# Running sums, sums of squares and the last residual's additions moved from GpSimd to VectorE in a two-layer decoder trunk

## The chip, the cores and the metric

The kernel runs on one core of one Trainium2 chip. The metric is the device time of one execution in microseconds (us); the time of a kernel is the median of its runs. The core's engines work side by side: TensorE (PE in the profile, its weight loads PEld) multiplies, VectorE (DVE), ScalarE (ACT) and GpSimd (POOL) work elementwise, and SyncE (SP) issues the transfers. Each engine takes its own instructions in the order in which the program lists them.

## What is computed

A trunk of two layers over 512 tokens of width 1024, in fp32. Cut to what matters here:

```python
def layer_norm(x, g, b):
    mu = jnp.mean(xf, axis=-1, keepdims=True)
    var = jnp.mean(jnp.square(xf - mu), axis=-1, keepdims=True)
    y = (xf - mu) * lax.rsqrt(var + LN_EPS)
    return (y * g + b)

for layer in range(DEPTH):
    if layer % 2 == 0:
        mix = concat([s5_mixer(...), stick_breaking_attention(...)]) @ mix_w_out[i] + mix_b_out[i]
    else:
        # inside: GLU, causal depthwise convolution of width 31, layer_norm, silu, product
        mix = conformer_conv(x, ...)
    x = layer_norm(DEEPNORM_ALPHA * x + mix, ln1_g[layer], ln1_b[layer])
    ffn = sqrelu_mlp(x, ffn_w1[layer], ffn_b1[layer], ffn_w2[layer], ffn_b2[layer])
    x = layer_norm(DEEPNORM_ALPHA * x + ffn, ln2_g[layer], ln2_b[layer])
```

## The kernel before

The activations lie with features on the 128 partitions and tokens along the row: `X[0]` to `X[7]` are eight 128x512 tiles, and a layer norm's mean runs over partitions and tiles. It is therefore a product with a matrix of 1/1024 (`ones`) on TensorE, which leaves the mean on every partition. Each product of activations and weights is made of three passes over two-part splits of both operands (`whi`, `wlo` of the weights, `xh`, `xl` or `hh`, `hl` of the activations): ScalarE rounds the high part (`CAST`, or `ACTIVATE` for a normalised tile), and VectorE subtracts to get the low part (L91 for weights, L198 and L877 for activations).

Four of the layer norms run in this layout, in two halves of 256 tokens each (`HALVES`): norm a (behind the mixer of layer 0), b (behind its feed-forward block), c (inside the convolution module) and d (behind that module). The fifth norm works on transposed tiles and is not touched.

A half goes through these steps. `LN.add` (L833) keeps a running sum `s` over the eight tiles as they come, seven additions of 128x256; those for tiles 1 to 6 are on GpSimd, the one for tile 7 on VectorE. `LN.norm` sends the sum through TensorE (`mp`, L841), subtracts the mean from the eight tiles on VectorE, squares them on ScalarE (`sq`), adds the squares up (tiles 0 to 3 by three additions on GpSimd at L853, tiles 4 to 7 by three on VectorE), and sends both partial sums through TensorE (`vp`). Then come the reciprocal root on ScalarE (`r`) with a refinement on VectorE (`t`), and in `ln_to_x` a scaling of each tile (`X<-X,PV,r`) and its split (`xh` on ScalarE, `xl` on VectorE at L877).

TensorE is given other work meanwhile. `tail_norm_lead` runs the second half's products of the block before (`Tail`, tiles `tla`, `tlb`, `tld`) while the first half is normalised, and the first half's products of the next block (`Lead`, tiles `fl` or `pl`) while the second half is. The lists `BEFORE` and `LEAD` say how many, and `tc.issue_after` pins the `ones` products behind them; the remaining order on each engine comes from a scheduler that places instructions as they become ready in its own estimate. Since TensorE takes its instructions in order, a `vp` product whose operand is late holds up what is listed behind it.

In the convolution module each channel tile's 31 taps are shared: TensorE takes some as diagonal products (`cv`, its diagonals `dh`, `dl` made on ScalarE), VectorE the others as multiply-adds into two accumulators (`cy`, `cz`, L339). The last two channel tiles are worked off in halves of tokens.

Behind norm d the feed-forward block of layer 1 begins: `fl` for its first six hidden tiles, then `f`. Beside it `residual` adds the two split parts of each normalised tile up again (L1098, eight additions of 128x512 on GpSimd), scales them on ScalarE, transposes them on TensorE (`xt`), and the second product of the block (`g`) is added to them.

Of the kernel before, what the change touches and what calls it, by code (L numbers as in the profile page):

```python
# [9 lines left out]
F32 = mybir.dt.float32  # L10
# [3 lines left out]
ALU = mybir.AluOpType  # L14
# [6 lines left out]
KT = D // P  # L21
# [126 lines left out]
def kernel(ctx: ExitStack, tc: tile.TileContext, a: dict, out: bass.AP):  # L148
    nc = tc.nc
    act = Act(tc)  # L150
    V, S, G, PE = nc.vector, nc.scalar, nc.gpsimd, nc.tensor
# [4 lines left out]
    def const(shape, name, dt=F32):  # L156
        return cst.tile(shape, dt, tag=name, name=name)
# [4 lines left out]
    X = [const([P, T], f"X{j}") for j in range(KT)]  # L162
# [28 lines left out]
    def pv(n, i):  # L191
        if n == "mix_b_in":
            return PB[:, i : i + 1]
        return PV[:, vrow[n] + i : vrow[n] + i + 1]
# [38 lines left out]
    def mm(name):  # L233
        return psum("mm", name, MIX_BUFS[0])
# [46 lines left out]
    xs, w0, u0 = [], None, mm("u0")  # L281
# [52 lines left out]
    def tt(o, x, y, op):  # L334
        V.tensor_tensor(o, x, y, op=op)  # L335
        return o
# [365 lines left out]
    ys = []  # L702
# [83 lines left out]
    def nps(name):  # L786
        return nps_.tile([P, T], F32, tag="n", name=name)
# [7 lines left out]
    def tmp(name, dt=F32):  # L795
        return hid.tile([P, T], dt, tag="tmp", name=name, bufs=8)
# [25 lines left out]
    class LN:  # L822
# [5 lines left out]
        def add(self, j, ys, c0, c1):  # L828

            if j == 1:  # L830
                self.s[c0] = tmp(f"s{self.n}{c0}")[:, c0:c1]
            if j:
                (V if j == KT - 1 else G).tensor_tensor(self.s[c0], ys[0][:, c0:c1] if j == 1 else self.s[c0], ys[j][:, c0:c1], op=ALU.add)  # L833

        def colmean(self, srcs, c0, c1, nm, other):

# [7 lines left out]
        def norm(self, ys, c0, c1, others=(None, None)):  # L844

            mu = self.colmean([self.s[c0]], c0, c1, "m", others[0])
            sq = []
            for j, y in enumerate(ys):
                tt(y[:, c0:c1], y[:, c0:c1], mu, ALU.subtract)
                sq.append(tmp(f"sq{self.n}{c0}{j}")[:, c0:c1])  # L850
                act(sq[j], y[:, c0:c1], AF.Square)
            for j in (1, 2, 3):
                G.tensor_tensor(sq[0], sq[0], sq[j], op=ALU.add)  # L853
            tt(sq[4], sq[4], sq[5], ALU.add)
            tt(sq[6], sq[6], sq[7], ALU.add)
            tt(sq[4], sq[4], sq[6], ALU.add)
            var = self.colmean([sq[0], sq[4]], c0, c1, "v", others[1])
            r, t_ = tmp(f"r{self.n}{c0}")[:, c0:c1], tmp(f"t{self.n}{c0}")[:, c0:c1]
            rsqrt(r, t_, var)
            return r  # L860

    def rsqrt(r, t_, var):

        act(r, var, AF.Abs_reciprocal_sqrt, bias=eps_c)
        stt(t_, var, EPS, r, ALU.add, ALU.mult)
        tt(t_, t_, r, ALU.mult)
        stt(r, t_, -3.0, r, ALU.add, ALU.mult)
# [68 lines left out]
    def tail_norm_lead(xk, name, bias, g, b, lead_n, lead_name):  # L936

        ln = LN(name)
        t = Tail(xk, ln, bias)
        t.run(KT)  # L940
        xs = new_x(f"x{name}")
        lead = Lead(lead_n, xs, lead_name)
        ln_to_x(ln, *HALVES[0], g, b, xs, [lambda n=n: t.run(n) for n in BEFORE[:2]])
        t.run(2 * KT - t.done)
        ln_to_x(ln, *HALVES[1], g, b, xs, [lambda n=n: lead.run(n) for n in BEFORE[2:]])
        return xs, lead.finish()
# [25 lines left out]
    xs, first = tail_norm_lead(cat[4:8], "a", rb[0], ("ln1_g", 0), ("ln1_b", 0), LEAD, "fl0")  # L972
# [19 lines left out]
    xs, first = tail_norm_lead(hs, "b", rb[1], ("ln2_g", 0), ("ln2_b", 0), 4, "pl")  # L992
# [75 lines left out]
    for c0, c1 in HALVES:  # L1068
# [8 lines left out]
        ys = [x[0] for x in acc]  # L1077
# [13 lines left out]
    xs, first = tail_norm_lead(cs_, "d", None, ("ln1_g", 8), ("ln1_b", 8), LEAD, "fl1")  # L1091
# [3 lines left out]

    def residual():
        for j in range(KT):
            G.tensor_tensor(X[j], xs[j][0].bitcast(F32), xs[j][1].bitcast(F32), op=ALU.add)  # L1098
            act(X[j], X[j], AF.Identity, bias=pv("ffn_b2", 8 + j), scale=ALPHA)
        for f in range(2):  # L1100
            pss = [nps(f"xt{b}{f}") for b in range(4)]
            for b in range(4):
                for i in range(4):
                    PE.transpose(pss[b][:, i * P : (i + 1) * P], X[4 * f + i][:, b * P : (b + 1) * P], ident)
            for b in range(4):
                XT[2 * b + f] = X[4 * f + b]
                S.copy(X[4 * f + b], pss[b])
# [10 lines left out]
    for bi, nb in enumerate(FFN_BLOCKS[1]):  # L1118
        hs = ffn1(1, bi, k0, nb, xs, stp, first if bi == 0 else ())
        if bi == 0:  # L1120
            residual()
        if bi < len(FFN_BLOCKS[1]) - 1:
            for f in range(2):
                pss = [nps(f"g{bi}{f}{b}") for b in range(4)]
                for k in range(0, nb, 2):
                    wh, wl = W.next()
                    for b in range(4):
                        for kk in range(2):
                            hh, hl = (t_[:, b * P : (b + 1) * P] for t_ in hs[k + kk])
                            for i, (u, v) in enumerate(((hh, wh), (hl, wh), (hh, wl))):  # L1130
                                PE.matmul(pss[b], u, v[:, kk, :], start=k + kk == 0 and i == 0,  # L1131
                                          stop=k + kk == nb - 1 and i == 2)
                for b in range(4):
                    tt(XT[2 * b + f], XT[2 * b + f], pss[b], ALU.add)
        k0 += nb
# [65 lines left out]
```

## Time and profile before

| | before |
|---|---|
| median of 3 runs | 1237.97 us (1237.91 to 1237.98) |
| profiled execution | 1239.18 us, of which the span of its instructions 1237.40 us |
| TensorE busy | 1195.6 us (97% of the span) |
| VectorE busy | 779.3 us (63%) |
| ScalarE busy | 567.1 us (46%) |
| GpSimd busy | 107.1 us (9%) |

All times below count from the start of the span. Norm a lies at 255 to 303 us, norm b at 592 to 660, the convolution module at 650 to 843 with norm c from 791 on, and norm d at 820 to 889. A busy TensorE is not TensorE at its peak, since its matmuls overlap; what it loses shows in the steps between their starts, in its waits and in the granted clock (PEclk).

### The profile page before, as it was taken

Reading aid. Unit: us, or ns where it says so; the run is one execution under the profiler, and the core shown is the slowest. Engines: PE = TensorE matmul, PEld = TensorE weight load, DVE = VectorE, ACT = ScalarE, POOL = GpSimd, SP = SyncE. Lnnn points to the kernel's source line nnn. Section 1 sums busy time; section 2 is a strip of 40 time slices with the busy share of each in tenths; the row PEclk is TensorE's granted clock in tenths of the full one; section 3 lists DMA queues with packets and bytes.
Section 4 is the critical chain, followed back from the end, with each engine's and each line's share of the span. In section 5 each row is a group of like instructions: output and inputs, shape, how many; then the busy total and the mean of one; then the engine's idle time right before and its main releaser. Section 6 shows DMA issues by size and latency. Waiting matters only on the chain.

```text
span 1237.4 us, 16678 instructions
## 1 busy us (share of the span) xinstructions
PE 1195.6 (97%) x6559; PEld 1015.3 (82%) x6559; DVE 779.3 (63%) x1321; ACT 567.1 (46%) x1020; POOL 107.1 (9%) x145
## 2 busy tenths in 40 slices
PE   9899999999999999999999999699899999999997
PEld 7776777789888888888998889689898888888885
DVE  8998774578633434434398999999853443434446
ACT  7736575635523324224255766876562332323230
POOL 1001100131000000000140011123400000000000
PEclk9999999999999999999999999889899999999999
DMA  8510141241533223333133121012052232423211
GB/s 206 162 37 20 35 119 52 85 137 42 163 102 102 80 90 102 102 102 98 43 103 103 35 69 35 1 48 90 33 172 69 85 119 68 134 68 105 86 51 68
DMA packets 111662, 105.93 MB, mean 86 GB/s; under 512 B 9378, under 2 KB 99746, under 8 KB 111584
## 3 DMA queue, kind: packets, MB, share of 16 engines
q1 hardware_dynamic: 111424, 104.84, 27.0%
q8 instruction: 51, 0.84, 0.3%
q14 instruction: 27, 0.22, 0.1%
q10 hardware_dynamic: 160, 0.03, 0.0%
HBM read 100.66 MB, written 4.19 MB: 85 GB/s over the span
## 4 chain that ended last, share of the span: by engine, by line
PE 75%; DVE 16%; ACT 4%; DMA 3%; issue 2%; POOL 1%; DVEq 0%; SPq 0%; ACTq 0%; POOLq 0%
PE f L207 23%; PE g L1131 12%; PE acf L207 11%; PE fl L207 4%; PE h L1115 3%; PE tld L207 3%; DVE cz L339 3%; PE tlb L207 2%; PE cv L1030 2%; DVE wlo L91 2%; DVE cy L339 2%; PE pl L207 1%; PE pv L207 1%; PE pg L207 1%; DVE X L339 1%
## 5 line engine op out<-in xcount | busy, mean ns | idle before, releaser
L90 ACT CAST whi<-raw 128x1024 fp32r<-128x1024 f32 x176 | 183.9, 1049 | 396.9 <-PE f L207 112.1
L91 DVE TENSOR_TENSOR wlo<-raw,whi 128x1024 fp32r<-128x1024 f32 x176 | 219.4, 1251 | 221.7 <-ACT whi L90 221.1
L1131 PE MATMUL g<-whi,hh 128*128 128x512 f32 x208 | 81.5, 392 | 0.0
L1131 PE MATMUL g<-wlo,hh 128*128 128x512 f32 x208 | 81.5, 392 | 0.0
L1131 PE MATMUL g<-whi,hl 128*128 128x512 f32 x208 | 81.4, 391 | 0.0
L207 PE MATMUL f<-xdh,whi 128*128 128x512 f32 x208 | 80.9, 389 | 0.0
L207 PE MATMUL f<-xah,whi 128*128 128x512 f32 x208 | 80.9, 389 | 0.0
L207 PE MATMUL f<-xal,whi 128*128 128x512 f32 x208 | 80.9, 389 | 0.0
L207 PE MATMUL f<-xdh,wlo 128*128 128x512 f32 x208 | 80.9, 389 | 0.0
L207 PE MATMUL f<-xdl,whi 128*128 128x512 f32 x208 | 80.9, 389 | 0.0
L207 PE MATMUL f<-xah,wlo 128*128 128x512 f32 x208 | 80.9, 389 | 0.0
L207 PE MATMUL acf<-hl,whi 128*128 128x512 f32 x192 | 75.2, 392 | 0.0
L207 PE MATMUL acf<-hh,whi 128*128 128x512 f32 x192 | 74.9, 390 | 0.0
L207 PE MATMUL acf<-hh,wlo 128*128 128x512 f32 x192 | 74.7, 389 | 0.0
L197 ACT CAST hh<-fr 128x512 fp32r<-128x512 f32 x64 | 39.7, 621 | 71.7 <-DVE fr L335 71.5
L198 DVE TENSOR_TENSOR hl<-fr,hh 128x512 fp32r<-128x512 f32 x64 | 44.2, 691 | 37.3 <-ACT hh L197 37.2
L339 DVE SCALAR_TENSOR_TENSOR cy<-hp,wdw,cy 128x512 f32<-128x512 f32 (+1 forms) x91 | 60.9, 678 | 0.1
L339 DVE SCALAR_TENSOR_TENSOR cz<-hp,wdw,cz 128x512 f32<-128x512 f32 (+1 forms) x86 | 59.9, 700 | 0.0
L1030 PE MATMUL cv<-hph,dh 128*128 128x256 f32 (+1 forms) x113 | 39.9, 353 | 10.0 <-ACT hph L197 8.3
L335 DVE TENSOR_TENSOR fr<-fr 128x512 f32<-128x512 f32 x64 | 43.8, 686 | 5.4 <-ACT fr L136 5.4
L1131 PEld LDWEIGHTS g<-whi,hl 128*128 128x128 f32 x208 | 39.1, 188 | 8.6
L1131 PEld LDWEIGHTS g<-wlo,hh 128*128 128x128 f32 x208 | 39.1, 188 | 8.6
(684 smaller groups left out, 3168.4 us busy)
## 6 DMA issues: line engine op xcount, KB each, us to landing
raw<-in_ffn_w_dram SPq DMA_DIRECT2D x48, 1024.0 KB, 5.4
raw<-in_ffn_w_dram SPq DMA_DIRECT2D x32, 512.0 KB, 3.5
raw<-in_conv_w_pw_dram SPq DMA_DIRECT2D x12, 1024.0 KB, 5.4
raw<-in_mix_w_in_dram SPq DMA_DIRECT2D x16, 512.0 KB, 4.0
xin<-in_x_dram SPq DMA_DIRECT2D x8, 256.0 KB, 4.1
raw<-in_s_w_glu_dram SPq DMA_DIRECT2D x4, 512.0 KB
raw<-in_mix_w_out_dram SPq DMA_DIRECT2D x4, 512.0 KB
raw<-in_mix_w_out_dram SPq DMA_DIRECT2D x2, 1024.0 KB
```

The source lines that it names most:

```text
L90: i0 = nc.scalar.copy(hi, raw).ins
L91: i1 = nc.vector.tensor_sub(lo, raw, hi.bitcast(F32)).ins
L197: i0 = S.copy(hi, src).ins
L198: i1 = V.tensor_sub(lo, src, hi.bitcast(F32)).ins
L207: ins = PE.matmul(ps[:, c0:c1], u[:, k, ksl], v[:, c0:c1], start=start and k == 0 and i == 0, stop=stop and k == n - 1 and i == 2).ins
L335: V.tensor_tensor(o, x, y, op=op)
L339: V.scalar_tensor_tensor(o, x, s, y, op0=op0, op1=op1)
L1030: PE.matmul(cps[j][:, c0:c1], u, v[:, t + c0 : t + c1], start=t == 0 and i == 0, stop=t == n - 1 and i == 2)
L1115: PE.matmul(ps, u, v, start=k == 0 and i == 0, stop=k == nk - 1 and i == 2)
L1131: PE.matmul(pss[b], u, v[:, kk, :], start=k + kk == 0 and i == 0, stop=k + kk == nb - 1 and i == 2)
```

## The change

The running sums are added on VectorE throughout. The squares are added in four pairs on VectorE, and all four results go through the `ones` product, where two did. The residual's eight additions are on VectorE. `tt` is the helper for a `tensor_tensor` on VectorE (its instructions stand under L335). Nothing else is edited; the scheduler's order follows.

```diff
@@ -830,7 +830,7 @@
             if j == 1:
                 self.s[c0] = tmp(f"s{self.n}{c0}")[:, c0:c1]
             if j:
-                (V if j == KT - 1 else G).tensor_tensor(self.s[c0], ys[0][:, c0:c1] if j == 1 else self.s[c0], ys[j][:, c0:c1], op=ALU.add)
+                tt(self.s[c0], ys[0][:, c0:c1] if j == 1 else self.s[c0], ys[j][:, c0:c1], ALU.add)
 
         def colmean(self, srcs, c0, c1, nm, other):
 
@@ -849,12 +849,9 @@
                 tt(y[:, c0:c1], y[:, c0:c1], mu, ALU.subtract)
                 sq.append(tmp(f"sq{self.n}{c0}{j}")[:, c0:c1])
                 act(sq[j], y[:, c0:c1], AF.Square)
-            for j in (1, 2, 3):
-                G.tensor_tensor(sq[0], sq[0], sq[j], op=ALU.add)
-            tt(sq[4], sq[4], sq[5], ALU.add)
-            tt(sq[6], sq[6], sq[7], ALU.add)
-            tt(sq[4], sq[4], sq[6], ALU.add)
-            var = self.colmean([sq[0], sq[4]], c0, c1, "v", others[1])
+            for j in range(0, KT, 2):
+                tt(sq[j], sq[j], sq[j + 1], ALU.add)
+            var = self.colmean(sq[::2], c0, c1, "v", others[1])
             r, t_ = tmp(f"r{self.n}{c0}")[:, c0:c1], tmp(f"t{self.n}{c0}")[:, c0:c1]
             rsqrt(r, t_, var)
             return r
@@ -1095,7 +1092,7 @@
 
     def residual():
         for j in range(KT):
-            G.tensor_tensor(X[j], xs[j][0].bitcast(F32), xs[j][1].bitcast(F32), op=ALU.add)
+            tt(X[j], xs[j][0].bitcast(F32), xs[j][1].bitcast(F32), ALU.add)
             act(X[j], X[j], AF.Identity, bias=pv("ffn_b2", 8 + j), scale=ALPHA)
         for f in range(2):
             pss = [nps(f"xt{b}{f}") for b in range(4)]
```

The first place is VectorE behind the second half of norm d. `rd` is the reciprocal root, `xdh` and `xdl` are the split parts, `X_61` to `X_68` the eight tiles. Before, the end of its scaling and splitting reads:

```order
L339 SCALAR_TENSOR_TENSOR X_66<-X_66,PV,rd_8432 128x256
L339 SCALAR_TENSOR_TENSOR X_67<-X_67,PV,rd_8432 128x256
L339 SCALAR_TENSOR_TENSOR X_68<-X_68,PV,rd_8432 128x256
L877 SCALAR_TENSOR_TENSOR xdl_8031<-X_64,PV,xdh_8030 128x256
L877 SCALAR_TENSOR_TENSOR xdl_8033<-X_65,PV,xdh_8032 128x256
L877 SCALAR_TENSOR_TENSOR xdl_8035<-X_66,PV,xdh_8034 128x256
L877 SCALAR_TENSOR_TENSOR xdl_8037<-X_67,PV,xdh_8036 128x256
L877 SCALAR_TENSOR_TENSOR xdl_8039<-X_68,PV,xdh_8038 128x256
L91 TENSOR_TENSOR wlo_8513<-raw_7802,whi_8512 128x1024
```

With the change the same place reads:

```order
L874 SCALAR_TENSOR_TENSOR xdl_8031<-X_64,PV,xdh_8030 128x256
L874 SCALAR_TENSOR_TENSOR xdl_8033<-X_65,PV,xdh_8032 128x256
L874 SCALAR_TENSOR_TENSOR xdl_8035<-X_66,PV,xdh_8034 128x256
L339 SCALAR_TENSOR_TENSOR X_67<-X_67,PV,rd_8432 128x256
L339 SCALAR_TENSOR_TENSOR X_68<-X_68,PV,rd_8432 128x256
L335 TENSOR_TENSOR X_61<-xdh_8024,xdl_8025 128x512
L874 SCALAR_TENSOR_TENSOR xdl_8037<-X_67,PV,xdh_8036 128x256
L874 SCALAR_TENSOR_TENSOR xdl_8039<-X_68,PV,xdh_8038 128x256
L335 TENSOR_TENSOR X_62<-xdh_8026,xdl_8027 128x512
L91 TENSOR_TENSOR wlo_8513<-raw_7802,whi_8512 128x1024
```

The first residual addition (`X_61`) now stands ahead of the last two splits, the second right behind them; the other six are listed later, in pairs behind the first three `fr` squarings of the feed-forward block. The last five splits no longer wait behind all the scalings.

The second place is VectorE in the second half of norm c, between the subtraction of the mean and the refinement, as a piece of the difference.

```order
+L335 TENSOR_TENSOR sqc_7690<-sqc_7690,sqc_7693 128x256
+L335 TENSOR_TENSOR sqc_7696<-sqc_7696,sqc_7699 128x256
 L335 TENSOR_TENSOR sqc_7702<-sqc_7702,sqc_7705 128x256
-L91 TENSOR_TENSOR wlo_7765<-raw_7762,whi_7764 128x1024
 L335 TENSOR_TENSOR sqc_7708<-sqc_7708,sqc_7711 128x256
 L91 TENSOR_TENSOR wlo_7769<-raw_7762,whi_7768 128x1024
-L335 TENSOR_TENSOR sqc_7702<-sqc_7702,sqc_7708 128x256
 L91 TENSOR_TENSOR wlo_7775<-raw_7772,whi_7774 128x1024
```

The four pair sums stand together, ahead of the weights' low parts (`wlo`) between which the three additions of before were spread.

The third place is TensorE at the variance of the second half of norm b; `pl` is the next block's first product. Before:

```order
L207 MATMUL pl_5808<-xbl_5444,whi_5199 128x256
L207 MATMUL pl_5808<-xbh_5443,wlo_5200 128x256
L841 MATMUL vpb_5833<-sqb_5754,ones 128x256
L841 MATMUL vpb_5833<-sqb_5766,ones 128x256
L207 MATMUL pl_5866<-xbh_5429,whi_5203 128x256
L207 MATMUL pl_5866<-xbl_5430,whi_5203 128x256
```

With the change:

```order
L207 MATMUL pl_5806<-xbh_5443,wlo_5200 128x256
L841 MATMUL vpb_5831<-sqb_5754,ones 128x256
L841 MATMUL vpb_5831<-sqb_5760,ones 128x256
L841 MATMUL vpb_5831<-sqb_5766,ones 128x256
L841 MATMUL vpb_5831<-sqb_5772,ones 128x256
L207 MATMUL pl_5866<-xbh_5429,whi_5203 128x256
```

Four `ones` products stand where two stood; in norms a and c, where the two stood apart, the four stand together too, or with one product between the last two (first half of c).

## Rows read from the trace of the kernel before

**Rows 1.** The page: busy time and instructions of engines; granted clock in 40 slices.

```profile
PE 1195.6 (97%) x6559; PEld 1015.3 (82%) x6559; DVE 779.3 (63%) x1321; ACT 567.1 (46%) x1020; POOL 107.1 (9%) x145
...
DVE  8998774578633434434398999999853443434446
...
PEclk9999999999999999999999999889899999999999
```

**Rows 2.** Busy time of each engine in four stretches, with clock (PEclk) and transfers.

```profile
254.00:302.00 48.00, 45.09 (x353) 43.56 (x353) 38.91 (x84) 19.39 (x40) 14.50 (x18) 1.00 0.24 77
...
715.00:780.00 65.00, 65.00 (x411) 58.76 (x410) 64.90 (x98) 46.06 (x131) 11.99 (x10) 1.00 0.15 49
...
780.00:806.00 26.00, 14.86 (x78) 12.99 (x77) 25.39 (x66) 21.81 (x61) 3.77 (x5) 0.77 0.00 1
...
881.00:891.00 10.00, 5.62 (x23) 4.63 (x24) 10.00 (x12) 6.44 (x11) 8.06 (x6) 0.75 0.00 0
```

**Rows 3.** The chain that ended last, around two second halves: start, length, what.

```profile
296.12 1.28 DVE X L339 x3
...
319.09 10.91 PE f L207 x48
...
876.11 1.28 DVE X L339 x3
...
908.33 10.91 PE f L207 x48
```

**Rows 4.** Timeline of VectorE behind the last layer norm: start, length, instruction.

```profile
877.30 2.31 DVE L877 SCALAR_TENSOR_TENSOR xdl<-X,PV,xdh 128x256 fp32r<-128x256 f32 x3
...
879.53 4.11 DVE L339 SCALAR_TENSOR_TENSOR X<-X,PV,rd 128x256 f32<-128x256 f32 x5
...
883.57 5.14 DVE L877 SCALAR_TENSOR_TENSOR xdl<-X,PV,xdh 128x256 fp32r<-128x256 f32 x5
```

**Rows 5.** Timeline of GpSimd: a running sum, then the residual additions.

```profile
778.88 1.73 POOL L833 TENSOR_TENSOR sc<-sc,cy 128x256 f32<-128x256 f32 x2 [9.32 <-DVE cy L335]
...
877.86 4.31 POOL L1098 TENSOR_TENSOR X<-xdh,xdl 128x512 f32<-128x512 f32 x3 [6.61 <-DVE xdl L877]
...
884.12 7.95 POOL L1098 TENSOR_TENSOR X<-xdh,xdl 128x512 f32<-128x512 f32 x5 [1.94 <-DVE xdl L877]
```

**Rows 6.** Timeline of VectorE: the convolution's taps.

```profile
722.54 1.23 DVE L339 SCALAR_TENSOR_TENSOR cy<-hp,wdw,cy 128x512 f32<-128x512 f32 x1
...
780.81 0.47 DVE L339 SCALAR_TENSOR_TENSOR cz<-hp,wdw,cz 128x256 f32<-128x256 f32 x1
...
810.67 0.97 DVE L339 SCALAR_TENSOR_TENSOR cz<-hp,wdw,cz 128x256 f32<-128x256 f32 x1
```

**Rows 7.** Timeline of VectorE: six additions or products of SBUF tiles in a row.

```profile
803.29 2.08 DVE L335 TENSOR_TENSOR cy<-cy,rc 128x256 f32<-128x256 f32 x6
```

**Rows 8.** Timeline of TensorE around variance products (two rows each, 128x256).

```profile
650.27 0.28 PE L207 MATMUL pl<-xbh,wlo 128*128 128x256 f32 x1
...
650.39 1.02 PE L841 MATMUL vpb<-sqb,ones 128*128 128x256 f32 x4
...
651.37 0.28 PE L207 MATMUL pl<-xbl,whi 128*128 128x256 f32 x1
...
825.44 0.70 PE L841 MATMUL vpc<-sqc,ones 128*128 128x256 f32 x2 [1.09 <-POOL sqc L853]
```

**Rows 9.** Waits of TensorE from 254 to 925 us: sum, times, longest.

```profile
PE fl L207 <- DVE xdl L877: 3.4, 4, 1.7
...
PE vpa L841 <- POOL sqa L853: 1.4, 2, 1.1
...
PE vpc L841 <- POOL sqc L853: 1.1, 1, 1.1
...
PE vpc L841 <- DVE sqc L335: 0.8, 1, 0.8
...
PE mpb L841 <- DVE sb L833: 0.6, 1, 0.6
```

## The prediction

> **What bounds the kernel now.** I read the page first: TensorE is busy for 97% of the span, VectorE for 63% and GpSimd for 9%; but VectorE's slices stand at 8 or 9 from about 620 to 900 us, and the granted clock leaves its full level only in three slices of the same stretch [rows 1]. So TensorE sets the end, and where it is not full, VectorE does. The busy times by stretch show where. From 715 to 780 us VectorE is busy for 64.90 of 65.00 us; from 780 to 806, still full (25.39 of 26), it leaves TensorE with 14.86 of 26; from 881 to 891 it is busy for all 10.00, TensorE for 5.62, at a clock of 0.75. In norm a (254 to 302) VectorE has 38.91 of 48 [rows 2]. TensorE's waits name the same places: 3.4 us for the low parts behind norm d (`xdl`), 1.4 for `sqa` and 1.1 for `sqc` on GpSimd, 0.8 for `sqc` on VectorE, 0.6 for `sb` [rows 9].
>
> The third view explains VectorE's long instructions. Behind norm d, eight scalings and eight splits of 128x256 take from 876.11 to 888.71 us: five scalings 4.11 us, five splits 5.14 [rows 3, 4]. In the same stretch GpSimd has its eight residual additions, 4.31 us for three and 7.95 for five [rows 5]. In the taps, an instruction of 0.47 us lasts 0.97 when GpSimd adds a running sum beside it [rows 5, 6]. So an addition on GpSimd is not free for VectorE: one of 128x256 lengthens a VectorE instruction by 0.5 us (0.97 less 0.47), one of 128x512 by about 1 us (five splits in 5.14 us, so 1.03 each, against 0.4 from start to start where three scalings take 1.28 [rows 3]). On VectorE itself an addition of 128x256 costs 2.08/6 = 0.35 us [rows 7]. The trade is 0.5 for 0.35 wherever VectorE is full.
>
> The Trainium skill's page "GPSIMD Engine Reference" (Specifications) says that GpSimd's way into SBUF is shared with VectorE and contended by VectorE instructions with two SBUF inputs. The lengthened splits and taps, with two such inputs, agree; the page gives no price.
>
> **The change, part by part.** VectorE takes 6 more sums and 1 more square addition in each of 8 halves, 56 of 128x256 (56 x 0.35 = 19.6 us), and 8 residual additions of 128x512, at most 2 x 0.35 = 0.7 us each (5.6 us). GpSimd stops altogether in these stages. What this does to the end depends on the stage.
>
> 1. The residual. From the second half's first scaling to the start of the first `f` product, norm d takes 908.33 - 876.11 = 32.22 us, norm a 319.09 - 296.12 = 22.97 [rows 3]. The two stretches have the same work, but for a lead of 72 products still listed behind the variance in d and 60 in a; at 0.12 us a product (650.27 to 650.39 [rows 8]) that is 1.4 us. In a, GpSimd is silent there. So its residual costs 32.22 - 22.97 - 1.4 = 7.8 us, part in VectorE's pace, part in the clock of 0.75 that follows TensorE's idling. Against this, one addition now stands ahead of the last two splits (0.7 us on a path of which TensorE still holds some cover): I count 0.3. Term: -7.5. Bounds: if the clock's share stays, only VectorE's own lengthening, 12.6 us less 16 x 0.4 = 6.2, less 0.7, that is -5.5; at most the whole difference, -9.2. The other six additions lie between squarings of the next block, where `f` is 16 us away.
>
> 2. The convolution and norm c. From 722.54 to 810.67 us twelve instructions are lengthened (the first and the last in [rows 6]), 12 x 0.5 = 6.0 us. In exchange come 12 sums and one square addition, 13 x 0.35 = 4.6. VectorE is full: -1.4. In the first half the last square addition no longer sits between taps, and with TensorE idle around it [rows 2] I count -0.7 (0 to -1.4). In the second half TensorE's waits of 1.1 + 0.8 us for the squares go [rows 9], since the four additions now stand together ahead of the weights' low parts; that chain then reaches the next product earlier too. I take -2.5 (bounds -1 to -3.5). Together -4.6.
>
> 3. Norms a and b. The waits of 1.4 and 0.6 us [rows 9] go for the most part; the queue takes 28 additions, in a on a VectorE that has 9 us free of 48 [rows 2], in b partly between products that it waits for anyway. I take -2.5 (+1 if the queue eats the gain, -3.5 if the first half's variance is also earlier).
>
> 4. Norm d ahead of its residual. TensorE waits there for nothing now, and 14 additions (4.9 us) replace lengthenings of some 3 us (about six of 0.5, at the price of rows 6): +0.6 (0 to +1.9).
>
> 5. Variance products. Two more per half. A group of two costs 651.37 - 650.27 less two steps of 0.12 = 0.86 us, and the second product of it takes half the 0.67 us between the group and the row behind it, 0.34 [rows 8]. Two more are +0.67 where the pair stood together (b, d), and less, about +0.47, where two groups of one become one group (a, c): 4 x 0.67 + 4 x 0.47 = 4.6. One of the latter falls on an idle TensorE (first half of c [rows 2]): +4.1 (3.1 to 5.4).
>
> Sum: -7.5 - 4.6 - 2.5 + 0.6 + 4.1 = -9.9 us. The profiled execution took 1239.18 us, 1.78 around its span of 1237.40, and is 1.2 us above the median of the runs; it would take 1229.3. For the median I predict 1237.97 - 9.9 = **1228 us**.
>
> **Rivals.**
>
> *The gain is given back in the same queue.* If TensorE waits for `f`'s weights or the hidden tiles because the residual additions stand ahead of them on VectorE, six of 0.7 us, 4.2 us, return: 1232. Against it: VectorE has 16 us from the last split to the first `f`, and its load there falls by the lengthened `wlo`.
>
> *More than the sum.* If norm c's chain, norms a and b and the clock all reach their good bounds (-9.2 - 6.3 - 3.5 + 4.1), it is 1223. For it: the waits of rows 9 are lower bounds, as a late product delays what follows.
>
> *Slower: VectorE becomes the bound.* If the long instructions are not GpSimd's doing and stay, all 64 additions come on top. In the full stretch from 715 to 811 us that is 13 x 0.35 = 4.6, in norms a, b and d, close to full, perhaps half of 42 x 0.35 = 14.7, so 7.4, behind norm d 0.7, and the products of step 5: 4.6 + 7.4 + 0.7 + 4.1 = +16.8, so 1255. It decides as soon as an addition on GpSimd lengthens VectorE by less than the 0.35 that it saves. Against it: each lengthened row of 4 and 6 lies beside a GpSimd row, and the same stretch behind norm a, without GpSimd, is 7.8 us shorter (step 1).
>
> [...]
>
> *No change to speak of.* The products of step 5 (4.1) and 1.5 us in the queues of norms a, b and d could meet a residual worth only 5.5 and a norm c worth 2: 1238 - 5.5 - 2 + 4.1 + 1.5 = 1236.
>
> **How the numbers follow.** Forecast 0.62 (1225 to 1231), given back 0.15, more 0.13, no change 0.06, slower 0.04. For the range I leave out the last two cases and the outer parts of the two next to the forecast: 1223 to 1234. A measurement of this kernel tells about 0.2% (2.5 us) from no change; so faster (under 1235.5) 0.90, same 0.06, slower 0.04.
>
> **What the profile after would show.** Step 1: eight scalings and eight splits behind norm d in about 7 us, no wait for `xdl` over 1 us, and a granted clock of 1.0 from 880 to 900 us. Step 2: no tap of 128x256 over 0.5 us, and no wait for `sqc` over 0.5. Step 3: no wait for `sqa` or `sb`. Step 5: eight groups of eight `ones` rows. GpSimd's last instruction lies before 250 us. I am wrong if VectorE's additions cost over 0.5 us each, if taps stay long without GpSimd, or if the scheduler's order makes TensorE wait at a new place, most likely where norm d's first half meets a full VectorE.

## The result, and the profile after

The changed kernel takes 1228.65 us (1227.07 to 1229.86, 4 runs), the kernel before 1237.94 beside it: a ratio of 0.9925, 95% interval 0.9908 to 0.9942. Measured again later (x9 below) it was 0.9928 (0.9914 to 0.9941). The profiled execution took 1229.86 us with a span of 1226.3.

The page after, busy time of engines, VectorE's slices and granted clock, to be read against [rows 1]:

```profile
PE 1194.0 (97%) x6591; PEld 1015.1 (83%) x6591; DVE 777.8 (63%) x1385; ACT 565.9 (46%) x1020; POOL 26.4 (2%) x65
...
DVE  7998774588634434434488999999762443434446
...
PEclk9999999999999999999999999899999999999998
```

VectorE has 64 instructions more and is busy 1.5 us less. From slice to slice its load has hardly changed. The clock leaves its full level in one slice of the stretch from 620 to 900 us instead of three. The stretches of [rows 2], by busy time of each engine in windows (PE, PEld, DVE, ACT, POOL, clock, transfers):

```profile
254.00:302.00 48.00, 47.22 (x372) 46.33 (x373) 42.52 (x99) 20.07 (x41) 0.00 (x0) 1.00 0.24 75
715.00:780.00 65.00, 65.00 (x416) 59.00 (x415) 64.23 (x109) 46.44 (x135) 0.00 (x0) 1.00 0.14 46
780.00:806.00 26.00, 15.51 (x85) 13.52 (x84) 25.52 (x70) 22.74 (x63) 0.00 (x0) 0.82 0.00 1
881.00:891.00 10.00, 10.00 (x86) 10.00 (x85) 8.47 (x11) 7.56 (x12) 0.00 (x0) 1.00 0.48 157
```

From 881 to 891 us TensorE is busy throughout at full clock, where it had 5.62 of 10 us at 0.75. From 780 to 806 little has changed: VectorE is still full, and TensorE stands for 7.8 us in a wait for ScalarE's `hph` (8.3 before), which ScalarE makes from VectorE's `hp`. What has changed in the convolution is the longest tap (shortest, middle and longest in ns, from 715 to 815 us), before and after:

```profile
L339 DVE SCALAR_TENSOR_TENSOR cz<-hp,wdw,cz x64: 469/744/1236, 715.5 to 814.7; 128x512 f32<-128x512 f32 x39, 128x256 f32<-128x256 f32 x25
...
L339 DVE SCALAR_TENSOR_TENSOR cz<-hp,wdw,cz x66: 478/745/764, 714.5 to 814.5; 128x512 f32<-128x512 f32 x39, 128x256 f32<-128x256 f32 x27
```

Before, eleven taps of `cy` and `cz` took 0.94 to 1.24 us, each beside an addition on GpSimd; after, none of 128x512 takes over 0.76 and none of 128x256 over 0.50. Next VectorE's timeline behind norm d (start, length, instruction), against [rows 4]:

```profile
871.94 1.28 DVE L339 SCALAR_TENSOR_TENSOR X<-X,PV,rd 128x256 f32<-128x256 f32 x3
873.13 1.27 DVE L874 SCALAR_TENSOR_TENSOR xdl<-X,PV,xdh 128x256 fp32r<-128x256 f32 x3
874.32 1.27 DVE L339 SCALAR_TENSOR_TENSOR X<-X,PV,rd 128x256 f32<-128x256 f32 x3
875.51 1.28 DVE L874 SCALAR_TENSOR_TENSOR xdl<-X,PV,xdh 128x256 fp32r<-128x256 f32 x3
876.70 0.88 DVE L339 SCALAR_TENSOR_TENSOR X<-X,PV,rd 128x256 f32<-128x256 f32 x2
877.49 0.69 DVE L335 TENSOR_TENSOR X<-xdh,xdl 128x512 f32<-128x512 f32 x1
878.09 0.88 DVE L874 SCALAR_TENSOR_TENSOR xdl<-X,PV,xdh 128x256 fp32r<-128x256 f32 x2
```

Eight scalings, eight splits and the first residual addition take 7.03 us (871.94 to 878.97), where scalings and splits took 12.60. The chain that ended last has no VectorE row there any more (against [rows 3]):

```profile
870.02 26.28 PE fl L207 x216
896.30 10.91 PE f L207 x48
907.21 3.56 PE xt L1101 x32
```

From the first scaling to `f` it is now 896.30 - 871.94 = 24.36 us, against 32.22 before. The waits of [rows 9] are gone but for 0.2 us of `vpc`; TensorE's longest ones from 254 to 925 us are now these (sum, times, longest). They are not new: before, the first stood at 8.3 us, one for `dh` in place of `dl` at 1.8, and the third at 0.9.

```profile
PE cv L1027 <- ACT hph L197: 7.8, 1, 7.8
...
PE cv L1027 <- ACT dl L136: 1.4, 1, 1.4
...
PE tla L207 <- ACT whi L90: 0.9, 1, 0.9
```

What has become longer is the variance products. TensorE's timeline in norm d's second half, against [rows 8]:

```profile
868.13 1.89 PE L841 MATMUL vpd<-sqd,ones 128*128 128x256 f32 x8
869.67 0.47 PE L207 MATMUL fl<-xdh,whi 128*128 128x256 f32 x1
```

From the group's start to the next row it is 1.54 us; before, at the same place, 0.67 (873.02 to 873.69).

Where the 11.1 us between the two spans came from shows in the starts of the same rows in TensorE's two timelines. TensorE's work left behind the two rows of variance products is nearly the same: 267 `tld` products behind that of c before and 264 after, and 216 `fl` products between that of d and the first `f` in both.

| place | before | after | shift |
|---|---|---|---|
| first `tla` (norm a begins) | 254.94 | 254.69 | -0.25 |
| first `f` behind norm a | 318.93 | 317.41 | -1.52 |
| first `cv` (behind norm b) | 666.41 | 665.32 | -1.09 |
| first `tld` (behind the first half of c) | 805.42 | 803.13 | -2.29 |
| variance products of c, second half, done | 829.76 | 825.08 | -4.68 |
| variance products of d, second half, done | 873.69 | 869.67 | -4.02 |
| first `f` behind norm d | 908.16 | 896.14 | -12.02 |
| first `h` | 1196.17 | 1184.22 | -11.95 |
| end of the span | 1237.40 | 1226.30 | -11.10 |

Most of it, 8.0 us, comes at one place, behind norm d; 3.6 in the convolution and norm c; norm a gives 1.3, norm b loses 0.4, and norm d ahead of its residual loses 0.7.

### The profile page after: what moved, and what is told of

It is laid out like the page before. It is cut to its first block, busy times and chain, and to the rows that moved or that the text cites. A ratio compares the mean times of both kernels' runs of the same rounds, so it can differ in the third digit from the quotient of the medians.

```text
span 1226.3 us, 16644 instructions
## 1 busy us (share of the span) xinstructions
PE 1194.0 (97%) x6591; PEld 1015.1 (83%) x6591; DVE 777.8 (63%) x1385; ACT 565.9 (46%) x1020; POOL 26.4 (2%) x65
## 4 chain that ended last, share of the span: by engine, by line
PE 81%; DVE 11%; ACT 4%; DMA 3%; issue 1%; POOL 0%; DVEq 0%; SPq 0%; POOLq 0%; ACTq 0%
PE f L207 23%; PE g L1128 12%; PE acf L207 11%; PE fl L207 6%; PE tld L207 4%; PE tlb L207 4%; PE cv L1027 3%; PE h L1112 3%; PE pv L207 2%; PE pg L207 2%; PE pl L207 2%; DVE cz L339 2%; DMA raw<-in_mix_w_in_dram 2%; PE acmo L207 1%; PE av L691 1%; DVE cy L339 1%
## 5 line engine op out<-in xcount | busy, mean ns | idle before, releaser
L91 DVE TENSOR_TENSOR wlo<-raw,whi 128x1024 fp32r<-128x1024 f32 x176 | 214.6, 1224 | 220.2 <-ACT whi L90 218.7
L339 DVE SCALAR_TENSOR_TENSOR cz<-hp,wdw,cz 128x512 f32<-128x512 f32 (+1 forms) x86 | 57.1, 666 | 0.0
L335 DVE TENSOR_TENSOR fr<-fr 128x512 f32<-128x512 f32 x64 | 43.7, 685 | 5.4 <-ACT fr L136 5.4
L1128 PEld LDWEIGHTS g<-whi,hh 128*128 128x128 f32 x208 | 39.1, 188 | 8.5
```

What stands on the lines that cost most here:

```text
L91: i1 = nc.vector.tensor_sub(lo, raw, hi.bitcast(F32)).ins
L339: V.scalar_tensor_tensor(o, x, s, y, op0=op0, op1=op1)
```

## The experiments

The theory: GpSimd's additions lengthen VectorE's instructions beside them; behind norm d this stands on the path to TensorE, in the norms and the convolution less so; and the two more products are a price of their own. The rivals are named with each run.

| run | median, us | ratio to before, interval | first scaling of d to `f`, us |
|---|---|---|---|
| before | 1238.63 / 1238.42 / 1237.73 (beside x1 to x4, x5 to x8, x9 to x11) | | 32.22 |
| x9, the changed kernel again | 1228.82 | 0.9928 (0.9914 to 0.9941) | 24.36 |
| x1, residual only | 1230.19 | 0.9942 (0.9928 to 0.9955) | 24.36 |
| x2, all but the residual | 1234.98 | 0.9973 (0.9964 to 0.9982) | 31.41 |
| x3, residual on GpSimd, late | 1236.83 | 0.9986 (0.9977 to 0.9994) | 25.07 |
| x4, additions beside the splits | 1236.22 | 0.9982 (0.9973 to 0.9991) | 32.64 |
| x5, squares to two | 1225.40 | 0.9893 (0.9877 to 0.9909) | |
| x10, squares to two, again | 1225.61 | 0.9901 (0.9887 to 0.9914) | |
| x6, squares to one | 1231.14 | 0.9942 (0.9929 to 0.9955) | |
| x7, running sums only | 1236.54 | 0.9985 (0.9976 to 0.9995) | 32.00 |
| x8, squares only | 1236.58 | 0.9984 (0.9976 to 0.9993) | 31.45 |
| x11, squares to two, four in c | 1223.98 | 0.9887 (0.9873 to 0.9900) | |

The medians of the three sessions are best compared by their ratios to before. The last column is read as in the prediction's step 1. The lead behind the variance is 72 products in these rows; in x5, x6, x10 and x11 it differs, so they have none.

**x1 and x2: the residual apart from the rest.** x1 is the kernel before with this edit alone; x2 is the changed kernel with it undone.

```diff
-            G.tensor_tensor(X[j], xs[j][0].bitcast(F32), xs[j][1].bitcast(F32), op=ALU.add)
+            tt(X[j], xs[j][0].bitcast(F32), xs[j][1].bitcast(F32), ALU.add)
```

> The kernel before, with only the eight residual additions moved to VectorE. In the changed kernel the stretch from the last variance product of norm d to the first f product is 8.0 us shorter. Theory (GpSimd's additions lengthen VectorE's splits behind norm d, and TensorE waits for these): nearly all of this comes back with this one line, so about 1230 us (1229 to 1231.5), eight scalings and eight splits in about 7 us, and everything ahead of norm d's variance as before. Rival (the gain comes from the running sums and squares, which let norm d begin earlier with more lead left): this line alone gives less than 4 us, so over 1234.

> The changed kernel with the eight residual additions back on GpSimd; running sums and squares stay on VectorE. Theory: the residual's 8 us is lost again, of which nothing depends on the other two parts: about 1236 us (1234.5 to 1237), with lengthened splits behind norm d. Rival (the parts do not add up, since the sums and squares have already freed the stretch): under 1233.

Both came out as the theory had it. In x1 the chain that ended last reads as in the changed kernel, with nothing else of the change in place:

```profile
872.24 26.42 PE fl L207 x216
898.66 10.91 PE f L207 x48
```

From its first scaling at 874.30 that is 24.36 us, to the hundredth the changed kernel's. In x2 the stretch is 31.41. The parts add up within their intervals: 1 - 0.9942 and 1 - 0.9973 make 0.85%, the whole change gave 0.75%.

**x3: the same additions on GpSimd, but behind the splits.** Is it that GpSimd is slow, or that it works beside the splits?

```diff
-        for j in range(KT):
-            G.tensor_tensor(X[j], xs[j][0].bitcast(F32), xs[j][1].bitcast(F32), op=ALU.add)
+        last = None
+        for j in reversed(range(KT)):
+            ins = G.tensor_tensor(X[j], xs[j][0].bitcast(F32), xs[j][1].bitcast(F32), op=ALU.add).ins
+            if last:
+                tc.add_manual_dep(ins, last, NOSYNC, reason="behind the last split")
+            last = ins.name
```

> The kernel before, its residual still on GpSimd, but in reversed order of tiles, so that all eight additions come behind the last split of norm d; everything else as before. Theory (what costs is that the additions lie beside the splits): the eight scalings and eight splits take about 7 us, not 12.6, no wait for the last split over 1 us, and some 6 to 8 us are gained although GpSimd does the same eight additions: 1230 to 1232. The additions then lengthen low parts of weights and squarings, which nothing waits for. Rival (GpSimd is too slow for the residual, wherever it lies, or TensorE's clock falls for another reason): 1236 to 1239, since the additions end some 6 us later still.

The mechanism came out; the time, 1236.83, did not, and lies in the rival's range. VectorE's timeline:

```profile
877.27 1.28 DVE L339 SCALAR_TENSOR_TENSOR X<-X,PV,rd 128x256 f32<-128x256 f32 x3
...
880.84 1.27 DVE L877 SCALAR_TENSOR_TENSOR xdl<-X,PV,xdh 128x256 fp32r<-128x256 f32 x3
...
883.08 0.88 DVE L877 SCALAR_TENSOR_TENSOR xdl<-X,PV,xdh 128x256 fp32r<-128x256 f32 x2 [0.18 <-ACT xdh L136]
884.42 6.48 DVE L91 TENSOR_TENSOR wlo<-raw,whi 128x1024 fp32r<-128x1024 f32 x3 [0.45 <-ACT whi L90]
890.82 1.78 DVE L335 TENSOR_TENSOR fr<-fr 128x512 f32<-128x512 f32 x1
```

and GpSimd's:

```profile
884.05 15.36 POOL L1099 TENSOR_TENSOR X<-xdh,xdl 128x512 f32<-128x512 f32 x8 [11.63 <-DVE xdl L877]
```

Scalings and splits are done in 6.7 us, and `f` starts 25.07 us behind the first scaling (at 902.17 in the timeline; the chain puts a run of `f` 0.17 later, as with 896.14 and 896.30 above). So 7.15 of the 7.86 us are won with GpSimd still adding. But the lengthening has moved to what comes next: three low parts of weights take 6.48 us, in x1 3.49, and a squaring 1.78 instead of 0.68. I had written that nothing waits for these. The chain that ended last says otherwise:

```profile
886.35 4.54 DVE wlo L91 x2
...
906.89 4.66 DMA raw<-in_ffn_w_dram
911.63 1.06 ACT whi L90
912.71 1.24 DVE wlo L91
913.97 3.55 DMA raw<-in_ffn_w_dram
...
919.78 1.14 PE xt L1108 x8
920.92 45.60 PE g L1135 x192
```

By this chain a late `wlo` frees its `raw` buffer late, so the next weights land late; ScalarE waits for them in its queue, and behind them stand the copies of `xt` that TensorE needs to go on. ScalarE's timeline adds a wait for GpSimd's late result in the same queue:

```profile
889.84 0.73 ACT L136 ACTIVATE X<-X,PV 128x512 f32<-128x512 f32 x1 [1.51 <-POOL X L1099]
```

No run tells the share of this wait, which is the rival's lateness, from that of the lengthened `wlo`. Among TensorE's waits from 895 us on:

```profile
PE xt L1108 <- ACT X L1111: 3.9, 1, 3.9
```

From 918 to 925 us its granted clock is 0.76, a mean of its two levels, behind that idle time, and the first block of `g` takes 45.60 us, where x1 has 43.94. 3.9 + 1.66 = 5.6 us go back. So the rival is wrong about the splits and the clock behind norm d (1.00 from 870 to 900 us), and I was wrong that GpSimd's additions would be free anywhere in this stretch.

**x4: GpSimd's additions put back as work that nobody reads.**

```diff
+        du = hpage("du", F32)
         for j in range(KT):
+            G.tensor_tensor(du, xs[j][0].bitcast(F32), xs[j][1].bitcast(F32), op=ALU.add)
             tt(X[j], xs[j][0].bitcast(F32), xs[j][1].bitcast(F32), ALU.add)
```

> The changed kernel, with eight additions of the same operands on GpSimd besides, into a scratch tile that nothing reads (work added, the result is not touched). Theory (an addition on GpSimd lengthens VectorE's instructions beside it): splits of about 1 us and scalings of over 0.4 us return behind norm d, and with them 5 to 8 us: 1234 to 1237. Rival (it was the lateness of the residual's results, or the order of VectorE's instructions): no change from the changed kernel, 1227 to 1230.

1236.22, a ratio of 0.9982 where the changed kernel has 0.9928 (x9): 0.54%, 6.7 us of the gain, are given back. VectorE's timeline, with the same order of instructions as above:

```profile
873.95 2.31 DVE L874 SCALAR_TENSOR_TENSOR xdl<-X,PV,xdh 128x256 fp32r<-128x256 f32 x3
876.18 3.32 DVE L339 SCALAR_TENSOR_TENSOR X<-X,PV,rd 128x256 f32<-128x256 f32 x3
879.42 2.29 DVE L874 SCALAR_TENSOR_TENSOR xdl<-X,PV,xdh 128x256 fp32r<-128x256 f32 x3
881.63 2.90 DVE L339 SCALAR_TENSOR_TENSOR X<-X,PV,rd 128x256 f32<-128x256 f32 x2
```

GpSimd's timeline in the same stretch:

```profile
874.56 4.26 POOL L1096 TENSOR_TENSOR du<-xdh,xdl 128x512 f32<-128x512 f32 x3 [634.84 <-DVE xdl L874]
880.03 4.21 POOL L1096 TENSOR_TENSOR du<-xdh,xdl 128x512 f32<-128x512 f32 x3 [1.22 <-DVE xdl L874]
```

Since nothing reads `du`, lateness and order are ruled out: what costs is that the addition runs at the same time. Beside the first three, VectorE is longer by 2.31 + 3.32 - 1.27 - 1.27 = 3.09 us, so 1.03 for each. The Trainium skill's page "GPSIMD Engine Reference" (Specifications), with its way into SBUF that is shared with VectorE and contended by VectorE instructions with two SBUF inputs, agrees with this: the lengthened rows have two such inputs. The Trainium skill's page "Perfetto Trace Analysis" (Optimizing Scalar/DVE Operations) says that offloading a saturated VectorE to GpSimd may make sense, but goes on that the two share a read port of SBUF, so that offloading between them might not help. This run, with 6.7 us given back, and x2, 0.45% over the changed kernel, are such cases.

**x7 and x8: running sums and squares one at a time**, each alone in the kernel before. x7 has

```diff
-                (V if j == KT - 1 else G).tensor_tensor(self.s[c0], ...
+                V.tensor_tensor(self.s[c0], ...
```

and x8

```diff
-            for j in (1, 2, 3):
-                G.tensor_tensor(sq[0], sq[0], sq[j], op=ALU.add)
...
+            for j in range(0, KT, 2):
+                tt(sq[j], sq[j], sq[j + 1], ALU.add)
+            var = self.colmean(sq[::2], c0, c1, "v", others[1])
```

> The kernel before, with only the running sums on VectorE (squares as before, residual on GpSimd). All but the residual gave 0.9973 of before, some 3.3 us. Theory (running sums free VectorE of lengthenings of 0.5 us at a price of 0.35 us, and cost TensorE nothing): about 2 us of it, 1235 to 1238, with the waits for the squares on GpSimd still there. Rival (the running sums gain nothing or lose, since VectorE is full, and all comes from the squares): 1238 or more.

> The kernel before, with only the squares in four pairs on VectorE and four products (running sums and residual on GpSimd as before). Theory: the waits for squares on GpSimd go (1.4, 1.1 and 0.8 us) and norm c's second half ends about 2 us earlier, but the products cost some 5.6 us, so no gain: 1237 to 1241. Rival (the squares carry the gain that is not the residual's): 1234 to 1236.

x7 came out at 1236.54, 0.15% under before, with the waits for the squares on GpSimd still there (`vpc` 1.9 us, `vpa` 1.7). x8, at 1236.58, is 0.4 us under the lower end of my expectation and 0.6 over the rival's upper one: the squares gain some 2 us although their products cost more than I had counted. Together (x2) they give 0.27%, apart 0.15% and 0.16%; within intervals of 0.1% these add up. By stages they don't: from the first `tla` to the first `f` behind norm a, where before takes 63.99 us, x7 takes 63.82 and x8 64.50, but x2, with both, 62.65. Each alone leaves TensorE a wait there, 1.7 us for GpSimd's `sqa` in x7 and 0.7 for the running sum `sa` in x8.

**x5, x10, x6 and x11: how many operands.** x5 (and x10, the same kernel) adds the four sums of squares of the changed kernel down to two, x6 to one by `tt(sq[0], sq[0], sq[4], ALU.add)` behind it, and x11 to two in norms a, b and d, but leaves four in c.

```diff
-            var = self.colmean(sq[::2], c0, c1, "v", others[1])
+            for j in (0, 4):
+                tt(sq[j], sq[j], sq[j + 2], ALU.add)
+            var = self.colmean(sq[::4], c0, c1, "v", others[1])
```

> The changed kernel with two more additions per half on VectorE, which bring the four sums of squares down to two, so that two products instead of four give the variance. Theory (the two more products of step 5 are a price of their own): in the changed trace eight rows of these products take 1.54 us to the next row, in that of before four rows take 0.67, so 0.87 per half comes back in seven halves (in the first half of norm c TensorE is idle anyway), 6.1 us, less 16 more additions of 0.35 us on VectorE, of which only those where VectorE is full count, some 2 us: 1224 to 1226. Rival (the change owes part of its gain to the shorter chain of additions, so that the products wait again for later sums): 1228 to 1231, with waits of the variance products for the squares.

> As the run with two operands, with one addition more per half and one product instead of two. Theory: two rows take 0.35 us to the next, four 0.67, so another 0.3 us per half on TensorE, 2.2 us in all, against eight more additions of 0.35 and a chain longer by about 0.4 us: within 1.5 us of the run with two operands. Rival (the chain is now late): more than 1.5 us slower than the run with two operands, with waits for the squares.

> The kernel with two sums of squares again, beside the changed kernel on the same chip. If its gain of 3 us over the changed kernel is real: 1223.5 to 1226.5 and at least 2 us under the changed kernel here. If it was a matter of the chip: within 1 us of it.

> Two sums of squares in norms a, b and d, four in norm c. With two, the second half of norm c ended 1.7 us later against the changed kernel (last variance product at -2.96 instead of -4.68 us against before), since VectorE is full there; in norm d the shorter products gave 1.8 us. Theory (the price of an addition counts where VectorE is full, that of a product where TensorE is): the 1.7 us stay and most of norm d's gain with them, 0.5 to 1.5 us under the run with two everywhere: 1223 to 1225. Rival (what norm c's second half gains is waited for in norm d anyway, where the first tile's products stood only 0.4 us apart): the same as with two everywhere.

Two operands beat four: x10 is 3.2 us under the changed kernel on the same chip (1225.61 and 1228.82), and x5 and x10 lie where the theory had them. TensorE's timeline of x5 in norm d's second half shows the price of the two products returned, 0.67 us to the next row instead of 1.54:

```profile
868.16 1.02 PE L841 MATMUL vpd<-sqd,ones 128*128 128x256 f32 x4
868.83 0.47 PE L207 MATMUL fl<-xdh,whi 128*128 128x256 f32 x1
```

One operand does not: 5.7 us over x5, where I had set 1.5 as the bound. The chain of additions is now late, but not as I had written it: TensorE does not wait for the squares, since their product is listed later; the lead runs out before the normalised tiles are there. TensorE's waits in x6 from 254 to 925 us:

```profile
PE fl L207 <- ACT xah L136: 3.0, 2, 2.1
PE pl L207 <- ACT xbh L136: 2.5, 1, 2.5
PE xt L1104 <- ACT X L1107: 1.8, 1, 1.8
```

In x5 the first two are 1.2 and 1.0. Behind the third the first block of `g` takes 45.63 us, as in x3, but the weights are not late this time. From the first scaling of norm d to the `xt` product that waits it is 42.51 us in x3 (877.27 to 919.78), but 36.92 in x6 (875.37 to 912.29) and 36.52 in x5 (871.10 to 907.62). TensorE is early: in x6 186 `fl` products are left behind the variance, in x5 201.

x11 takes 1223.98 us, the fastest here: 4.8 us under the changed kernel on the same chip, and 14 under before. Against x10 it is 1.6 us by the medians. Its four runs (1222.95 to 1224.73) all lie under the four of x10 (1224.92 to 1226.38), but the intervals of the ratios overlap and the profiled spans differ by 0.3 (1222.9 and 1223.2). Norm c's last variance products are done at 823.25 us in x11 and at 826.35 in x10, yet the first `f` behind norm d starts at 892.88 and 893.07. This is not the rival's waiting: in neither run does TensorE's list of waits have one in between. It has more `tld` products left behind norm c's variance, 264 in x11 and 241 in x10 (window; then PE, PEld and DVE busy on these tiles, clock, transfers):

```profile
823.20:892.80 69.60, 33.06 (x264) 32.23 (x264) 5.20 (x13) 1.00 0.29 94
...
826.30:893.00 66.70, 29.92 (x241) 29.30 (x241) 5.67 (x14) 1.00 0.26 80
```

At 0.12 us each the 23 products are 2.8 of the 3.1 us. So the variance of norm c only stands earlier in TensorE's list, and the premise of this expectation falls: the 1.7 us that norm c was to lose with two operands came of the same order, since x5 has 241 left, the changed kernel 264. Whether four in c pays at all stays open.

## Why the prediction was right

The forecast of 1228 with its range held the time, and the case forecast was the one that came. By its own steps:

**Step 1, the residual** (-7.5): measured -7.86 (32.22 to 24.36), in x1 the same. The comparison with norm a, 22.97 + 1.4 = 24.4, gave the new length of the stretch almost exactly. That the clock's share would go with it was right too: from 881 to 891 us it is 1.0. The 0.3 for the addition ahead of the last two splits was not needed: TensorE is never without work there.

**Step 2, convolution and norm c** (-4.6): from the first `cv` to the end of the variance products in c's second half the shift goes from -1.09 to -4.68, -3.6; with step 5's products in the second half taken out (0.84, below) -4.4. The taps went back to their short length, as expected. But the parts were off: of the 1.4 for VectorE's pace only 0.4 shows by the first mean (`mpc`, 792.38 to 790.90, so -1.48), since TensorE is full from 715 to 780 us before and after.

**Steps 3 and 4, norms a, b and d** (-2.5 and +0.6): the shifts are -1.27 in a, +0.43 in b, +0.66 in d. Without the products (1.90, 1.14 and 1.74) that is -3.2, -0.7 and -1.1: 5.0 in sum, 3.1 us better than the two terms. In norm a neither sums (x7) nor squares (x8) alone give it, only both.

**Step 5, variance products** (+4.1): this term was mis-sized. The trace of before has 0.35 + 0.24 us for two groups of one (norm a, 273.70 and 275.91), the changed one 1.54 for one group of four: +0.95 in each half of a, where I had 0.47. In d it is 1.54 - 0.67 = 0.87, where I had 0.67; in b 0.27 (before, the group at 627.62 took 1.27, with a wait of 0.3 for a square in it) and 0.87; in c's second half 1.54 - 0.70 = 0.84. Without c's first half, where TensorE is idle, that makes 5.6 us, beyond my bound of 5.4. I had taken 0.34 us for the second product of a pair as the price of a third and fourth; they cost 0.43 each.

**What no step had**: 0.25 us are won ahead of norm a, and behind the first `h` 0.85 are lost (-11.95 to -11.10). The first is within what differs from one execution to the next: the first `tla` starts at 253.17 us in x1 and at 256.22 in x3, whose edits lie behind norm d. Steps 3 and 4 erred by 3.1 us to one side and step 5 by 1.5 to the other. That the sum of -9.9 stood as close to the 9.3 us measured is therefore luck in part; step 1, the largest term, is not, since x1 and x4 test it by itself. Between the spans it is 11.1; the profiled execution after had 3.6 us outside its span, that of before 1.8, and the runs do not show why.

**The rivals.** The gain was not given back behind the splits: the added wait for `f`'s weights did not come. "Slower" hung on additions that lengthen VectorE by less than the 0.35 us they save; x4 measured 1.03 for one of 128x512, which on VectorE takes 0.6 (877.49 to 878.09 above), and the taps' 0.5 for one of 128x256 is gone from the changed kernel. "No change" and "more than the sum" did not come either, by a median of 1228.65.

## What to carry to other kernels

Where GpSimd shares elementwise work with a full VectorE, compare the length of VectorE's instructions beside GpSimd's with the same ones elsewhere: here an addition put on GpSimd cost VectorE more than doing it. Before an earlier start is called a gain, count the work that is left behind it: the 3.1 us of x11 in norm c were order. Before a stage is judged, look for its twin in the same trace that lacks the suspect; norm a gave norm d's length to 0.1 us. An addition more on VectorE against a product less on TensorE has an optimum that neither engine's load alone shows: four, two and one operand took 0.9928, 0.9901 and 0.9942 of before here, so try the neighbours. Part of what one operand costs is again order, since its products are listed later and leave less work behind them.

## What the runs showed of the hardware that was not expected

- An addition of 128x512 on GpSimd lengthened the VectorE instruction beside it by about the same 1.0 to 1.1 us, whatever that one's size: scalings and splits of 128x256 (x4), a squaring of 128x512 (0.68 to 1.78, x3) and low parts of 128x1024 (two in 4.54 us against 1.22 each, x3). All of these have two inputs in SBUF. One of 128x256 lengthened taps of both sizes by 0.5 (before: 0.47 to 0.97 and 0.74 to 1.24).
- Four `ones` products in a row (after) held up TensorE for 1.54 us, two (before, x5) for 0.67, one (before) for 0.24 to 0.35.
- The last row of `h` starts 9.0 to 9.1 us ahead of the span's end in the changed kernel and in x1, x5, x6, x9, x10 and x11, but 8.4 to 8.5 us before and in x2, x3, x4, x7 and x8. This went with GpSimd being silent behind norm d, not with the residual on VectorE, which x4 has too; why, no run shows.
